# Gated DeltaNet layer on one core: decay matrices and gate vectors spread over the partitions by DMA from DRAM, in place of TensorE transposes

## The chip, the cores and the metric

The kernel runs on one core of a Trainium2 chip. The metric is the device time of one execution in microseconds, as the median of several runs.

## What is computed

One decoder layer in float32, over 256 positions of width 2048: a gated DeltaNet token mixer and a SwiGLU channel mixer, each followed by a layer norm, with gates, scales and shifts from a conditioning vector `c`. The mixer has 16 query/key heads and 32 value heads of width 128. The reference, cut to the parts near the change:

```python
mod = (cond @ mod_w[i] + mod_b[i])[:, None, :]
sh1, sc1, ga1, sh2, sc2, ga2 = jnp.split(mod, 6, axis=-1)
h = x * (1 + sc1) + sh1
y = gated_deltanet(h, ...)
x = layer_norm(ALPHA_DN * x + (1 + ga1) * y, ln_g[i, 0], ln_b[i, 0])
h = x * (1 + sc2) + sh2
y = swiglu(h, ffn_w_gu[i], ffn_w_down[i])
x = layer_norm(ALPHA_DN * x + (1 + ga2) * y, ln_g[i, 1], ln_b[i, 1])

# in the mixer, per chunk and head
g = -jnp.exp(a_log) * jax.nn.softplus(a + dt_bias)
gc = jnp.cumsum(g, -1)
diff = gc[..., :, None] - gc[..., None, :]
decay = jnp.where(lower, jnp.exp(jnp.where(lower, diff, 0.0)), 0.0)
L = jnp.where(strict, jnp.einsum('bhnid,bhnjd->bhnij', kb, k) * decay, 0.0)
sol = lax.linalg.triangular_solve(L + I, rhs, left_side=True, lower=True, unit_diagonal=True)
a_qk = jnp.where(lower, jnp.einsum('bhnid,bhnjd->bhnij', q, k) * decay, 0.0)
```

The kernel works with two chunks of 128 positions (c = 0, 1).

## The kernel before

**The products.** Every large product is split in three: each weight tile is divided into a high part `wh` (ScalarE, L190) and a low part `wl` (VectorE, L191), the activations likewise, and TensorE runs three 128x512 products per pair of tiles (L223 to L225). A `Group` makes 512 output columns; a `chunk` of it is four row tiles of the weight for both halves of the positions, 24 products. `pos` counts chunks, and all times of the plan ("units") are in chunks. Weights come by DMA through the queue of SyncE (SP).

**The stages.** First the conditioning scales `sc1`, `sh1` and the transposed, scaled input `hT` are made while the first projections already run. Then the projections of q/k, v and z follow, quarter by quarter (`q` = 0 to 3; a quarter is four query/key heads and eight value heads). Then w_out, the first layer norm (`ln1`), the feed-forward products (w_gu, then w_down) and the last norm.

**Tasks beside the stream.** The mixer's own work is written as generators. `spawn(t, gen)` puts one on a heap at plan time t, `advance` runs whatever is due and gives its instructions the priority of that time; a `yield d` moves the task d units on. The language's planner then orders the instructions of each engine by these priorities and by its own estimate of when operands are ready. On the chip each engine runs its queue in that fixed order. The constants in lines 35 to 39 are such distances.

**The mixer of a quarter.** `gates` (L410) makes `beta` and the cumulated log decays `gc` (positions on partitions, a column for each chunk and head), `ngc` = -gc and the exponentials. `qk_done` and `v_done` spawn the convolutions; `v_done` of the second half also spawns `gdn(q)`. `gdn` waits until q's norms are there and until the states of quarter q-1 are done (`state_ends`), takes the tile `LA` (one buffer, 128 x 16 x 2 x 128: for each chunk and head the matrix of the solve and the matrix a_qk), and spawns four `la_task`s. Each handles one chunk and four heads:

- ScalarE writes `dg` = gc of a head down the columns plus a matrix `below` of -1e30 under the diagonal (L543), four Identity activations of 128x128;
- TensorE transposes it (L547, four transposes into a `gd` PSUM buffer);
- ScalarE makes the decay `dm` = Exp(transpose + ngc) (L551);
- TensorE makes the k.k and k.q products `pk` (L556), and VectorE multiplies them by `dm` and the row scales into LA (L561).

`solve_task` then inverts the triangular matrices in place (VectorE's long loop, then products of LA's blocks), and `state_task` runs the two chunks through the state; its last operation is L686. `dg` and `dm` share the tag `V` (3 buffers) with the state's tiles.

**The tail of the mixer.** When a quarter's states end, `fo` follows (a `pow` on GpSimd, L718), z's gate is applied (L795), and `o_task` transposes and splits the results into the operands `oT` of w_out (L817, L818). These take the places of tiles that have become free: `oTa` those of `kq`, `oTb` that of `LA`, and so on.

**Gate vectors.** `gate_row` (L831) turns a gate, held as 128 x 16 columns (`ga1`, `ga2`), into a row of 2048 on all partitions: for each column a TensorE transpose of the broadcast column (L838), 16 in all, and four ScalarE copies (L839). It is called for `ga1` ahead of w_out and for `ga2` ahead of w_down; `residual` reads the row (L845). `mods_late` makes `ga1` and `ga2` from streamed weights (`macc`, L272).

GpSimd's queue holds few instructions: the `pow` for `rn` and `fo`, a MEMSET and a COPY that prepare X of the solve, and the DMAs of small or repeated tensors.

Of the kernel before, what the change touches and what calls it, by code (L numbers as in the profile page):

```python
# [8 lines left out]
F32 = mybir.dt.float32  # L9
# [7 lines left out]
D = 2048  # L17
# [12 lines left out]
def gdn_layer_kernel(ctx: ExitStack, tc: tile.TileContext, x, c, mod_w, mod_b, ln_g, ln_b,  # L30
# [7 lines left out]
    GDN, LAGAP, LA1, LA2, LA3, SOLVE, HOP = 3.0, 0.5, 0.3, 0.6, 1.5, 5.4, 0.6  # L38
# [82 lines left out]
    below = consts.tile([128, 128], F32, name="below")  # L121
    ts(below, jp, 0.0, -1e30, op0=OP.is_gt, op1=OP.mult)
# [282 lines left out]
    negc = consts.tile([128, 32], F32, name="negc")  # L405
    XN = gp.tile([64, 16, 64], F32, name="XN", tag="XN", bufs=1)
# [3 lines left out]
    def gates(ps):  # L410
# [37 lines left out]
        ts(ngc, gc, -1.0, None, op0=OP.mult)  # L448
        act(egc, gc[:, 1, :], AF.Exp)
# [5 lines left out]
    oq, fo, LA, omq, state_done, state_ends = {}, {}, {}, {}, {}, set()  # L455

# [78 lines left out]

    def la_task(q, c, g, sc):

        kqq, hv, la = kq[q], q * 8, LA[q]
        s0 = c * 8 + g * 4
        dg = gp.tile([128, 4, 128], F32, name="dg", tag="V", bufs=3)  # L540
        for i in range(4):
            h = hv + g * 4 + i
            act(dg[:, i, :], below, AF.Identity, bias=gc[:, c, h:h + 1])  # L543
        yield LA1
        pb = gd()
        for i in range(4):
            tr(pb[:, i * 128:(i + 1) * 128], dg[:, i, :], ident)  # L547
        dm = gp.tile([128, 4, 128], F32, name="dm", tag="V", bufs=3)
        for i in range(4):
            h = hv + g * 4 + i  # L550
            act(dm[:, i, :], pb[:, i * 128:(i + 1) * 128], AF.Exp, bias=ngc[:, c, h:h + 1])  # L551
        yield LA2
        pk = gd()
        for n in range(2):
            nn = g * 2 + n
            mm(pk[:, n * 256:(n + 1) * 256], kqq[:, nn, 0, c * 128:(c + 1) * 128],  # L556
               kqq[:, nn, :, c * 128:(c + 1) * 128], start=True, stop=True)
        for i in range(4):
            h = g * 4 + i
            src = pk[:, (i // 2) * 256:(i // 2 + 1) * 256].rearrange("p (a b) -> p a b", a=2)  # L560
            stt(la[:, s0 + i], src, sc[:, 0, c, h:h + 1], dm[:, i, None, :].to_broadcast([128, 2, 128]),  # L561
                op0=OP.mult, op1=OP.mult)

# [127 lines left out]
    def gdn(q):  # L691


        while q not in rq2 or q and q - 1 not in state_ends:
            yield 0.2
        hv, rk, rq = q * 8, rk2[q], rq2[q]
        LA[q] = gp.tile([128, 16, 2, 128], F32, name="LA", tag="LA", bufs=1)
# [3 lines left out]
        tt(sc[:, 1, 0], sc[:, 0, 0], kse[:, hv:hv + 8], op=OP.mult)  # L701
        for c in range(2):
            for g in range(2):
                spawn(now[0] + LAGAP * (2 * c + g), la_task(q, c, g, sc))
# [24 lines left out]
    def qk_done(q, which):  # L729
        nat = []  # L730

        def done(t, ps, n=None):
            nat.append(evac(t, ps) if n is None else n)
            if t == 0:
                return
            both = []
            ss = work.tile([128, 2, 4], F32, name="ss", tag="ss", bufs=2)
            t1 = conv_start()
            for h in (0, 2):
                spawn(t1 + PAIR / 2 * h, qk_pair(q, which, nat, h, ss, both))  # L740
            spawn(t1 + PAIR + SILU + 0.6, qk_norm(q, which, ss, both))
        return done
# [88 lines left out]
    def gate_row(tag, cols, name):  # L831

        row = held.tile([128, D], F32, name=name, tag=tag)
        for g in range(4):
            p = tp()
            for i in range(4):
                k = 4 * g + i
                tr(p[:, i * 128:(i + 1) * 128], cols[:, k:k + 1].to_broadcast([128, 128]), ident)  # L838
            act(row[:, g * 512:(g + 1) * 512], p, AF.Copy)  # L839
# [58 lines left out]
    with at(n - 4):  # L898
# [7 lines left out]
        gates(pp)  # L906

# [216 lines left out]
```

## Time and profile before

| | us |
|---|---|
| median of the runs shown | 1728.11 (three runs, 1725.67 to 1729.37) |
| the profiled execution's own time | 1724.8 |
| span of the profile, first to last instruction | 1723.0 |
| TensorE busy | 1668.4 |
| VectorE busy | 1140.0 |
| ScalarE busy | 879.3 |
| GpSimd busy | 49.0 |

In the profile PE is TensorE, PEld its weight loads, DVE is VectorE, ACT ScalarE, POOL GpSimd and SP SyncE; a trailing q is an engine's queue. A line such as L547 is a line of the kernel before. "out<-in" names the tile that is written and those that are read. Records of products overlap, because the array is pipelined, so the sum of their durations is more than the time they take. "Idle before" is time for which the engine waited ahead of an instruction, with what ended it.

### The profile page before, as it was taken

Reading aid. Unit: us, or ns where it says so; the run is one execution under the profiler, and the core shown is the slowest. Engines: PE = TensorE matmul, PEld = TensorE weight load, DVE = VectorE, ACT = ScalarE, POOL = GpSimd, SP = SyncE. Lnnn points to the kernel's source line nnn. Section 1 sums busy time; section 2 is a strip of 40 time slices with the busy share of each in tenths; the row PEclk is TensorE's granted clock in tenths of the full one; section 3 lists DMA queues with packets and bytes.
Section 4 is the critical chain, followed back from the end, with each engine's and each line's share of the span. In section 5 each row is a group of like instructions: output and inputs, shape, how many; then the busy total and the mean of one; then the engine's idle time right before and its main releaser. Section 6 shows DMA issues by size and latency. Waiting matters only on the chain.

```text
span 1723.0 us, 23257 instructions
## 1 busy us (share of the span) xinstructions
PE 1668.4 (97%) x8685; PEld 1325.3 (77%) x8685; DVE 1140.0 (66%) x1641; ACT 879.3 (51%) x1426; POOL 49.0 (3%) x58
## 2 busy tenths in 40 slices
PE   5999999999999999999999999999999999999996
PEld 2666777787887878787788778888878887888885
DVE  2466988958966988847776865764567444455455
ACT  2433669769568667564333734444444443433331
POOL 0000000001001000000000000000000000000000
PEclk8999999999999999999999999999999999999998
DMA  9998785535863777747888576886678666765653
GB/s 351 364 337 282 225 290 186 171 111 160 257 205 112 245 247 240 247 147 237 300 285 278 159 259 193 298 271 188 187 243 290 186 190 204 249 195 190 196 193 107
DMA packets 183938, 390.82 MB, mean 227 GB/s; under 512 B 12096, under 2 KB 14320, under 8 KB 182800
## 3 DMA queue, kind: packets, MB, share of 16 engines
q1 hardware_dynamic: 181808, 378.64, 67.5%
q0 software_dynamic: 2016, 10.68, 1.8%
q8 instruction: 68, 1.11, 0.3%
q14 instruction: 46, 0.38, 0.1%
HBM read 385.08 MB, written 4.19 MB: 226 GB/s over the span
## 4 chain that ended last, share of the span: by engine, by line
PE 71%; DVE 11%; DMA 8%; issue 5%; ACT 3%; POOL 1%; SPq 1%; DVEq 0%; POOLq 0%; ACTq 0%
PE pj L224 19%; PE pj L223 19%; PE pj L225 19%; DMA mraw<-in_mod_w_dram 6%; DVE wl L191 5%; DVE macc L272 1%; PE gd L225 1%; PE gd L224 1%; ACT wh L190 1%; PE gd L223 1%; PE tp L311 1%; DVE X L586 1%; DVE cy L470 1%; DVE tmp L584 1%; PE tp L1039 1%
## 5 line engine op out<-in xcount | busy, mean ns | idle before, releaser
L191 DVE TENSOR_TENSOR wl<-raw,wh 128x1024 fp32r<-128x1024 f32 x522 | 634.9, 1222 | 375.5 <-ACT wh L190 372.4
L190 ACT ACTIVATE wh<-raw 128x1024 fp32r<-128x1024 f32 x522 | 552.3, 1061 | 603.2 <-PE pj L225 480.9
L223 PE MATMUL pj<-wh,h2T 128*128 128x512 f32 x704 | 278.2, 395 | 0.0
L225 PE MATMUL pj<-wh,h2T 128*128 128x512 f32 x704 | 276.7, 393 | 0.0
L224 PE MATMUL pj<-wl,h2T 128*128 128x512 f32 x704 | 276.6, 393 | 0.0
L223 PE MATMUL pj<-wh,hT 128*128 128x512 f32 x640 | 256.9, 403 | 0.0
L224 PE MATMUL pj<-wl,hT 128*128 128x512 f32 x640 | 256.4, 401 | 0.1
L225 PE MATMUL pj<-wh,hT 128*128 128x512 f32 x640 | 256.2, 401 | 0.0
L272 DVE SCALAR_TENSOR_TENSOR macc<-mraw,cond,macc 128x1024 f32<-128x1024 f32 x120 | 153.4, 1278 | 55.8 <-DMA mraw<-in_mod_w_dram 55.4
L223 PEld LDWEIGHTS pj<-wh,h2T 128*128 128x128 f32 x704 | 132.8, 189 | 30.7 <-issue 1.6
L225 PEld LDWEIGHTS pj<-wh,h2T 128*128 128x128 f32 x704 | 132.7, 189 | 28.6 <-issue 0.8
L224 PEld LDWEIGHTS pj<-wl,h2T 128*128 128x128 f32 x704 | 132.7, 188 | 27.5 <-issue 0.8
L223 PEld LDWEIGHTS pj<-wh,hT 128*128 128x128 f32 x640 | 120.8, 189 | 26.6 <-issue 3.3
L225 PEld LDWEIGHTS pj<-wh,hT 128*128 128x128 f32 x640 | 120.9, 189 | 24.6 <-issue 1.2
L224 PEld LDWEIGHTS pj<-wl,hT 128*128 128x128 f32 x640 | 120.8, 189 | 24.4 <-DVE wl L191 0.9
L470 DVE SCALAR_TENSOR_TENSOR cy<-tp,cw,cy 128x255 f32<-128x255 f32 (+2 forms) x192 | 86.2, 476 | 1.3 <-ACT cy L466 1.2
L224 PE MATMUL gd<-wl,hT 128*128 128x512 f32 x128 | 51.5, 404 | 1.4 <-DVE wl L191 1.4
L223 PE MATMUL gd<-wh,hT 128*128 128x512 f32 x128 | 49.9, 398 | 2.0 <-DVE part L256 1.1
L225 PE MATMUL gd<-wh,hT 128*128 128x512 f32 x128 | 51.8, 408 | 0.0
L311 PE MATMUL tp<-mraw,cond 128*32 128x256 f32 x368 | 34.9, 464 | 11.1 <-DMA mraw<-in_mod_w_dram 11.1
L223 PE MATMUL pj<-wh,oTc 128*128 128x512 f32 x112 | 43.9, 392 | 0.0
L225 PE MATMUL pj<-wh,oTc 128*128 128x512 f32 x112 | 43.8, 391 | 0.0
(385 smaller groups left out, 2252.0 us busy)
## 6 DMA issues: line engine op xcount, KB each, us to landing
raw<-in_gdn_w_in_dram SPq DMA_DIRECT2D x194, 512.0 KB, 4.7
mraw<-in_mod_w_dram SPq DMA_DIRECT2D x192, 512.0 KB, 5.4
raw<-in_ffn_w_gu_dram SPq DMA_DIRECT2D x176, 512.0 KB, 4.4
raw<-in_ffn_w_down_dram SPq DMA_DIRECT2D x88, 512.0 KB, 4.7
raw<-in_gdn_w_out_dram SPq DMA_DIRECT2D x64, 512.0 KB, 5.0
x<-in_x_dram SPq DMA_DIRECT2D x8, 256.0 KB, 6.0
r<-in_x_dram POOLq DMA_DIRECT2D x2, 1024.0 KB, 5.1
x1s<-r POOLq DMA_DIRECT2D x2, 1024.0 KB, 6.7
```

Source lines behind the costliest of these rows:

```text
L190: act(hi, raw, AF.Copy)
L191: tt(lo, raw, f32(hi), op=OP.subtract)
L223: mm(ps, sh, wh, start=start, stop=False)
L224: mm(ps, sh, wl, start=False, stop=False)
L225: mm(ps, sl, wh, start=False, stop=stop)
L272: return stt(acc, w, cond[:, k:k + 1], acc, op0=OP.mult, op1=OP.add)
L311: mm(p[32 * j:32 * j + 32, 0:hw], cond[:, k:k + 1].to_broadcast([128, 32]), raw[:, kl, j * hw:(j + 1) * hw], start=(k == 0), stop=(k == KT ...
L470: stt(y[:, o + s:o + 256], p[:, o:o + 256 - s], tap(3 - s, ct + i), y[:, o + s:o + 256], op0=OP.mult, op1=OP.add)
L584: tt(tv, LD[:, j + 1:32, j:j + 1].to_broadcast([128, n, m]), X[:, j, None, 0:m].to_broadcast([128, n, m]), op=OP.mult)
L586: tt(X[:, j + 1:32, 0:m], X[:, j + 1:32, 0:m], tv, op=OP.subtract)
L1039: tr(p[:, i * 256 + t * 128:i * 256 + (t + 1) * 128], nats[j, t][:, (2 * i2 + i) * 128:(2 * i2 + i + 1) * 128], ident)
```

## The change

The decays come by another way. After `gc` is made, `gates` transposes it once (64 rows of 128: chunk and head by position), copies it to SBUF and writes it to a DRAM scratch `gcrows` by a DMA on the GpSimd queue. A new task `decay_task(q)`, spawned when q's second q/k group is done, waits for the end of the states of quarter q-1 and for the gates, takes the tile LA, and issues four DMAs on the GpSimd queue. Each reads four rows of `gcrows` and spreads them over all 128 partitions, straight into the a_qk half of LA. After LA1 units GpSimd masks each block in place (`affine_select`, -1e30 under the diagonal), and ScalarE applies the Exp in place, with `ngc` as bias. `la_task` keeps the products and the multiplication, which now reads the decay from LA itself; `dg`, its transposes, `dm` and `below` are gone. `gdn` waits for the first decay block of its quarter before it spawns the `la_task`s. The distances LA1, LA2 and LA3 change.

`gate_row` transposes the 128 x 16 columns once, copies 16 rows of 128 to SBUF, writes them to a DRAM scratch and reads them back as a row of 2048 on all 128 partitions; both DMAs are on the GpSimd queue.

```diff
--- before.py
+++ after.py
@@ -35,7 +35,7 @@
     SPLIT, MOD0, MODEVERY = 10, 30.0, 0.95
     MGAP, CGAP0, CGAP, CSTEP = 1.5, 1.0, 2.0, 2.3
     CONV, PAIR, SILU = 0.2, 0.4, 2.4
-    GDN, LAGAP, LA1, LA2, LA3, SOLVE, HOP = 3.0, 0.5, 0.3, 0.6, 1.5, 5.4, 0.6
+    GDN, LAGAP, LA1, LA3, SOLVE, HOP = 3.0, 0.5, 1.2, 0.8, 5.4, 0.6
     ALONE, MACW, ZW, OW = 1.5, 1.0, 0.1, 0.3
 
 
@@ -118,8 +118,6 @@
     ones = upper[:, 127:128]
     mhalf = consts.tile([128, 16], F32, name="mhalf")
     nc.vector.memset(mhalf, -0.5)
-    below = consts.tile([128, 128], F32, name="below")
-    ts(below, jp, 0.0, -1e30, op0=OP.is_gt, op1=OP.mult)
 
     pbit = work.tile([128, 1], I32, name="pbit", tag="gw0", bufs=1)
     nc.gpsimd.iota(pbit, pattern=[[0, 1]], base=0, channel_multiplier=1)
@@ -403,6 +401,7 @@
     ngc = consts.tile([128, 2, 32], F32, name="ngc")
     egc = consts.tile([128, 32], F32, name="egc")
     negc = consts.tile([128, 32], F32, name="negc")
+    gcrows = dram.tile([64, 128], F32, name="gcrows", tag="gcrows", bufs=1)
     XN = gp.tile([64, 16, 64], F32, name="XN", tag="XN", bufs=1)
     nc.gpsimd.memset(XN[0:32, :, 32:64], 0.0)
     kse = consts.tile([128, 32], F32, name="kse")
@@ -446,6 +445,12 @@
         mm(p[:, 64:96], ones.to_broadcast([128, 128]), q[:, 0, :], start=True, stop=True)
         nc.vector.tensor_copy(gc, p[:, 0:64].rearrange("p (a b) -> p a b", a=2))
         ts(ngc, gc, -1.0, None, op0=OP.mult)
+
+        pr = tp()
+        tr(pr[:64, 0:128], gc.rearrange("p a b -> p (a b)"), ident)
+        gr = work.tile([64, 128], F32, name="gr", tag="hf", bufs=2)
+        nc.vector.tensor_copy(gr, pr[:64, 0:128])
+        nc.gpsimd.dma_start(gcrows, gr)
         act(egc, gc[:, 1, :], AF.Exp)
         ts(negc, egc, -1.0, None, op0=OP.mult)
         tt(kse, p[:, 64:96], gc[:, 0, :], op=OP.subtract)
@@ -453,6 +458,7 @@
 
     kq, knat, rk2, rq2, ik2 = {}, {}, {}, {}, {}
     oq, fo, LA, omq, state_done, state_ends = {}, {}, {}, {}, {}, set()
+    has_gates, has_decay = [], set()
 
     def conv_silu(nat, h, ct, dst):
 
@@ -533,23 +539,29 @@
                 act(oq[q][:, c, hq + i, :], p[:, c * 256 + i * 128:c * 256 + (i + 1) * 128], AF.Copy,
                     scale=ik2[q][:, c, hq + i:hq + i + 1])
 
+    def decay_task(q):
+
+        while q and q - 1 not in state_ends or not has_gates:
+            yield 0.2
+        LA[q] = gp.tile([128, 16, 2, 128], F32, name="LA", tag="LA", bufs=1)
+        parts = [(c, g, LA[q][:, c * 8 + g * 4:c * 8 + g * 4 + 4, 1, :]) for c in range(2) for g in range(2)]
+        for c, g, dm in parts:
+            h0 = c * 32 + q * 8 + g * 4
+            nc.gpsimd.dma_start(dm, gcrows[None, h0:h0 + 4, :].to_broadcast([128, 4, 128]))
+        yield LA1
+        for c, g, dm in parts:
+            nc.gpsimd.affine_select(dm, dm, pattern=[[0, 4], [1, 128]], compare_op=OP.is_ge, fill=-1e30,
+                                    base=0, channel_multiplier=-1)
+            for i in range(4):
+                h = q * 8 + g * 4 + i
+                act(dm[:, i, :], dm[:, i, :], AF.Exp, bias=ngc[:, c, h:h + 1])
+            has_decay.add(q)
+            yield LAGAP
+
     def la_task(q, c, g, sc):
 
-        kqq, hv, la = kq[q], q * 8, LA[q]
+        kqq, la = kq[q], LA[q]
         s0 = c * 8 + g * 4
-        dg = gp.tile([128, 4, 128], F32, name="dg", tag="V", bufs=3)
-        for i in range(4):
-            h = hv + g * 4 + i
-            act(dg[:, i, :], below, AF.Identity, bias=gc[:, c, h:h + 1])
-        yield LA1
-        pb = gd()
-        for i in range(4):
-            tr(pb[:, i * 128:(i + 1) * 128], dg[:, i, :], ident)
-        dm = gp.tile([128, 4, 128], F32, name="dm", tag="V", bufs=3)
-        for i in range(4):
-            h = hv + g * 4 + i
-            act(dm[:, i, :], pb[:, i * 128:(i + 1) * 128], AF.Exp, bias=ngc[:, c, h:h + 1])
-        yield LA2
         pk = gd()
         for n in range(2):
             nn = g * 2 + n
@@ -558,8 +570,10 @@
         for i in range(4):
             h = g * 4 + i
             src = pk[:, (i // 2) * 256:(i // 2 + 1) * 256].rearrange("p (a b) -> p a b", a=2)
-            stt(la[:, s0 + i], src, sc[:, 0, c, h:h + 1], dm[:, i, None, :].to_broadcast([128, 2, 128]),
+            stt(la[:, s0 + i], src, sc[:, 0, c, h:h + 1], la[:, s0 + i, None, 1, :].to_broadcast([128, 2, 128]),
                 op0=OP.mult, op1=OP.mult)
+        return
+        yield
 
     def solve_task(q):
 
@@ -691,14 +705,15 @@
     def gdn(q):
 
 
-        while q not in rq2 or q and q - 1 not in state_ends:
+        while q not in rq2 or q not in LA:
             yield 0.2
         hv, rk, rq = q * 8, rk2[q], rq2[q]
-        LA[q] = gp.tile([128, 16, 2, 128], F32, name="LA", tag="LA", bufs=1)
         sc = work.tile([128, 2, 2, 8], F32, name="gsc", tag="gsc", bufs=2)
         tt(sc[:, 0], rk, rk, op=OP.mult)
         tt(sc[:, 0], sc[:, 0], beta[:, :, hv:hv + 8], op=OP.mult)
         tt(sc[:, 1, 0], sc[:, 0, 0], kse[:, hv:hv + 8], op=OP.mult)
+        while q not in has_decay:
+            yield 0.1
         for c in range(2):
             for g in range(2):
                 spawn(now[0] + LAGAP * (2 * c + g), la_task(q, c, g, sc))
@@ -739,6 +754,8 @@
             for h in (0, 2):
                 spawn(t1 + PAIR / 2 * h, qk_pair(q, which, nat, h, ss, both))
             spawn(t1 + PAIR + SILU + 0.6, qk_norm(q, which, ss, both))
+            if which == 1:
+                spawn(t1, decay_task(q))
         return done
 
     def v_done(q, half):
@@ -831,12 +848,13 @@
     def gate_row(tag, cols, name):
 
         row = held.tile([128, D], F32, name=name, tag=tag)
-        for g in range(4):
-            p = tp()
-            for i in range(4):
-                k = 4 * g + i
-                tr(p[:, i * 128:(i + 1) * 128], cols[:, k:k + 1].to_broadcast([128, 128]), ident)
-            act(row[:, g * 512:(g + 1) * 512], p, AF.Copy)
+        p = tp()
+        tr(p[:KT, 0:128], cols, ident)
+        rows = work.tile([KT, 128], F32, name="grow", tag="rows", bufs=2)
+        nc.vector.tensor_copy(rows, p[:KT, 0:128])
+        there = dram.tile([KT, 128], F32, name=f"{name}d", tag=name, bufs=1)
+        nc.gpsimd.dma_start(there, rows)
+        nc.gpsimd.dma_start(row, there.rearrange("k p -> (k p)")[None, :].to_broadcast([128, D]))
         return row
 
     def residual(row, g, t, ps, xin, st):
@@ -904,6 +922,7 @@
             mm(pp, wl, hh, start=False, stop=False)
             mm(pp, wh, hl, start=False, stop=(k == KT - 1))
         gates(pp)
+        has_gates.append(True)
 
     def late_mods():
         yield from mods_late(ga1, 32, 1.0, MODEVERY)
```

## Rows read from the trace of the kernel before

**Rows 1.** The page's head: span, then busy time, share and instructions of each engine.
```profile
span 1723.0 us, 23257 instructions
...
PE 1668.4 (97%) x8685; PEld 1325.3 (77%) x8685; DVE 1140.0 (66%) x1641; ACT 879.3 (51%) x1426; POOL 49.0 (3%) x58
```

**Rows 2.** Busy us by stretches: length, PE, PEld, DVE, ACT, POOL, clock, DMA share, GB/s.
```profile
258.00:301.00 43.00, 42.99 (x211) 34.39 (x210) 35.09 (x60) 42.70 (x92) 0.00 (x0) 1.00 0.60 190
...
516.00:559.00 43.00, 41.56 (x220) 33.45 (x219) 29.45 (x64) 37.01 (x104) 4.54 (x2) 1.00 0.40 118
...
1118.00:1161.00 43.00, 43.00 (x194) 35.28 (x193) 28.09 (x26) 18.40 (x20) 0.00 (x0) 1.00 0.83 278
```

**Rows 3.** Groups of instructions of TensorE and ScalarE: busy us, mean ns, idle before.
```profile
L547 PE MATMUL gd<-ident,dg 128*128 128x128 f32 x64 | 15.4, 278 | 0.0
...
L838 PE MATMUL tp<-ident,ga 128*128 128x128 f32 x32 | 4.6, 276 | 0.1
...
L543 ACT ACTIVATE dg<-below,gc 128x128 f32<-128x128 f32 x64 | 21.3, 407 | 0.0
L551 ACT ACTIVATE dm<-gd,ngc 128x128 f32<-128x128 f32 x64 | 19.0, 372 | 1.1 <-PE gd L547 1.0
```

**Rows 4.** Timeline of TensorE around one block of transposes: start, length.
```profile
250.88 0.39 PE L225 MATMUL pj<-wh,hT 128*128 128x512 f32 x1
251.11 0.60 PE L547 MATMUL gd<-ident,dg 128*128 128x128 f32 x4
...
251.78 0.40 PE L224 MATMUL pj<-wl,hT 128*128 128x512 f32 x1
```

**Rows 5.** Timeline of VectorE: quarter 0's decays and LA, then quarter 2's LA.
```profile
241.22 0.23 DVE L447 COPY gc<-tp 128x64 f32<-128x64 f32 x1 [0.79 <-PE tp L446]
...
278.58 1.65 DVE L561 SCALAR_TENSOR_TENSOR LA<-gd,gsc,dm 128x256 f32<-128x256 f32 x4
...
524.81 0.69 DVE L686 TENSOR_TENSOR oq<-gd,Qs 128x512 f32<-128x512 f32 x1 [1.94 <-PE gd L685]
...
532.57 1.66 DVE L561 SCALAR_TENSOR_TENSOR LA<-gd,gsc,dm 128x256 f32<-128x256 f32 x4 [0.74 <-PE gd L547]
...
541.86 1.65 DVE L561 SCALAR_TENSOR_TENSOR LA<-gd,gsc,dm 128x256 f32<-128x256 f32 x4
```

**Rows 6.** DMA issues: count, size of each, median us from issue to landing.
```profile
x1s<-r POOLq DMA_DIRECT2D x2, 1024.0 KB, 6.7
...
lrow<-in_ln_g_dram POOLq DMA_DIRECT2D x1, 1024.0 KB, 5.1
...
l<-in_ln_g_dram POOLq DMA_DIRECT2D x4, 256.0 KB, 8.6
```

**Rows 7.** Groups of GpSimd's instructions.
```profile
L509 POOL TENSOR_TENSOR rn<-ss,mhalf 128x8 f32<-128x8 f32 x8 | 15.2, 1894 | 233.7 <-DVE ss L507 196.0 <-DVE gsc L701 37.6
...
L578 POOL COPY X<-parity 128x16 f32<-128x16 f32 x8 | 2.8, 383 | 0.3
...
L1093 POOL DMA_DIRECT2D l<-in_ln_g_dram x4 | 2.1, 539 | 0.0
L576 POOL MEMSET X<- 128x512 f32 x4 | 2.1, 527 | 163.5 <-PE gd L610 160.0 <-PE tp L462 3.5
```

**Rows 8.** Timeline: w_out's first operand in LA's place is made, then read.
```profile
768.88 0.75 DVE L818 SCALAR_TENSOR_TENSOR oTb<-tp,nwc,oTb 128x512 fp32r<-128x512 f32 x1
...
781.12 0.48 PE L223 MATMUL pj<-wh,oTb 128*128 128x512 f32 x1
```

**Rows 9.** Instructions on the tile ga1row: ns min/median/max, first and last start.
```profile
L845 DVE TENSOR_TENSOR ry<-pj,ga1row x8: 680/684/691, 819.5 to 958.0; 128x512 f32<-128x512 f32 x8
L839 ACT ACTIVATE ga1row<-tp x4: 580/594/598, 791.3 to 794.5; 128x512 f32<-128x512 f32 x4
```

**Rows 10.** Timeline of VectorE and GpSimd from 422.9 us.
```profile
422.95 1.28 DVE L272 SCALAR_TENSOR_TENSOR macc<-mraw,cond,macc 128x1024 f32<-128x1024 f32 x1
423.12 2.61 POOL L509 TENSOR_TENSOR rn<-ss,mhalf 128x8 f32<-128x8 f32 x1 [10.26 <-DVE ss L507]
```

## The prediction

> **What bounds the kernel now.** The first view to open is the head of the page [rows 1]. The reader is to see that TensorE is busy 1668.4 of 1723.0 us, and that no other engine comes near it. A share over the whole span hides stages with other limits, so the second view is the busy time by stretches of 43 us [rows 2]. In the stretch from 258 us, where the first of the four quarters of heads is worked on, ScalarE is busy 42.70 of 43 us and TensorE 42.99. In the stretch from 516 us TensorE is busy 41.56 and ScalarE 37.01, with the DMA engines at 0.40. From 1118 us, in the feed-forward part, TensorE has no idle time at all. So the product stream on TensorE sets the pace in all stages that the change touches: an instruction taken out of that stream shortens the time by its place in the stream, and an instruction taken from another engine is worth nothing unless TensorE was waiting for it. All of TensorE's idle time is 1723.0 - 1668.4 = 54.6 us.
>
> **What a transpose costs in the stream.** The change takes out two groups of TensorE transposes, 64 of `dg` (L547) and 32 of the gate columns (L838). A record of one lasts about 0.276 us [rows 3], but records overlap, so that is not its price. The timeline shows the price [rows 4]: the product before a block of four starts at 250.88, the second product after it at 251.78, so 0.90 us hold two products and four transposes. A product alone takes 43.00 / 194 = 0.222 us (TensorE's row of the stretch from 1118, where nearly all instructions are such products). That leaves 0.90 - 0.444 = 0.456 us for four, 0.114 us for one.
>
> **The change, part by part.**
> *Removed in `la_task`.* 64 transposes: 64 x 0.114 = 7.3 us of stream. 64 Identity activations take 21.3 us of ScalarE [rows 3]; I count them at nothing, because even in the stretch from 258 us, with ScalarE full, TensorE idles only 0.01 us [rows 2]. The transposes also leave two uses of the `gd` PSUM buffers and of the `V` buffers; nothing in the rows shows TensorE waiting for these, so nothing is counted. The 64 Exp activations stay and read SBUF in place of PSUM; I take them as unchanged.
>
> *Removed in `gate_row`.* 32 transposes: 32 x 0.114 = 3.6 us. Eight ScalarE copies of about 0.59 us [rows 9] go too; they are hidden beside products.
>
> *Added on TensorE.* One transpose in `gates` and one in each `gate_row`: 3 x 0.114 = 0.3 us. Net of the stream: 7.3 + 3.6 - 0.3 = 10.6 us.
>
> *Added: gate vectors through DRAM.* A small write, then a 1 MB broadcast read. Nearest rows [rows 6]: 6.7 us for the 1 MB write of `x1s`, 5.1 us for the 1 MB broadcast of `ln_g`. Together at most 12 us. The vector used to begin at 791.3 and is first read at 819.5 [rows 9], 28 us later, so this lies under w_out's products; the second one, ahead of w_down, has the same kind of cover. Cost zero; without the cover it would be these 12 us once each.
>
> *Added: the decay path.* Once: a copy and a small DRAM write in `gates`. For each quarter: four DMA issues on the GpSimd queue, each spreading 4 rows of 512 B to 128 partitions (256 KB), four masks `affine_select` of 128x512 on GpSimd, then the Exps. For quarter 0 the sums `gc` are there at 241.22 and LA is first written at 278.58 [rows 5]: 37 us of cover, for a write of at most 6.7 us, a read of 5.1 to 8.6 us [rows 6] and the masks. It costs nothing there. Quarter 1 has no tight start either, because `gdn(1)` is spawned by the values' projection and not by the end of quarter 0.
>
> Quarters 2 and 3 are the tight ones: LA has one buffer, so the DMAs can start only when the states of the quarter before have read it. Before, states end at 524.81 + 0.69 = 525.5, LA is written from 532.57, and the last block from 541.86 [rows 5]: 16.4 us from free buffer to last block. After: four issues of 0.54 us (the `l` row of [rows 7]) are 2.2 us; landing takes 5.1 to 8.6 us, and I take the 8.6 of the rows with several 256 KB broadcasts issued together [rows 6], as here; then four masks of m each in a row, then four Exps of 0.372 us [rows 3], 1.5 us. In all 12.3 + 4m against 16.4: late by 4m - 4.1 us. No row shows a mask. Below it stands the MEMSET of the same 128x512, 0.527 us; above it the COPY of 16 strided columns, 0.383 us or 24 ns a column, which would make 12.3 us of 512 columns [rows 7]. I take m = 1 us, near the MEMSET, since the shape is the same and only a read is added. Then the path is as early as before (0.1 us), and the sum has no loss.
>
> What is queued behind these waits: on GpSimd the `pow` for `fo` and `rn` and the MEMSET of X; on VectorE, behind the first L561 that waits for a decay, the `wl` splits on which every product depends; on ScalarE, behind an Exp that waits for a mask, the `wh` splits. So a decay that is really late doesn't stay beside the stream, it stops it. The dues also move: LA1 is now 1.2 units after the states' end, and LA3 falls from 1.5 to 0.8, which puts the solve 0.7 unit earlier where the decays are ready in time, and about 0.6 later for quarters 2 and 3. At the very end there is cover: the first operand of w_out that takes LA's place is complete at 768.88 + 0.75 = 769.6, and TensorE reads it at 781.12 [rows 8], 11.5 us later; past that, a late quarter 3 would stop w_out.
>
> *Added DMA bytes.* 16 x 256 KB and 2 x 1 MB are 6 MB; in the stretch from 516 us the DMA engines are busy 0.40 of the time, so the weights keep their lead. The longer GpSimd work is 16 masks on an engine busy for 49.0 us in all [rows 1].
>
> **The sum.** 1724.8 us is the profiled execution's own time (span 1723.0 and 1.8 around it). 1724.8 - 10.6 = 1714.2. The median of the runs shown, 1728.1, lies 3.3 above that execution, so the forecast for a median is 1728.1 - 10.6 = 1717.5.
>
> **A rule weighed.** GpSimd's `pow` for `rn` that starts at 423.12, inside VectorE's `macc` of 422.95 to 424.23, lasts 2.61 us against a mean of 1.894 [rows 7, 10]: a GpSimd operation that meets a VectorE operation with two SBUF inputs is longer by 0.7 us or more. The Trainium skill ("SBUF — State Buffer", section "SBUF: two separate sides") says that the port pair which the two engines share is locked by whichever starts first for the whole instruction, against a VectorE operation with two SBUF inputs too, and that the other one is blocked until then. By that rule each mask can wait out one VectorE operation, and the time would be the second rival's 1727.5 in place of 1717.5; the row agrees as far as GpSimd's side goes, and no row here shows VectorE held.
>
> **The rivals.**
> *Larger gain (chance 0.09).* The transposes are worth the busy time that their rows show, and not their place: 15.4 + 4.6 = 20.0 us [rows 3], less three new ones (0.7 us), 19.3 us: 1708.8. For it: ScalarE full at 258 us. Against it: the 0.90 us of [rows 4].
>
> *Masks and VectorE hold each other (0.14).* Each mask waits out one `macc` of 1.28 us [rows 10]: m = 2.28 us, late by 4 x 2.28 - 4.1 = 5.0 us in each of two quarters, 10.0 us together. Nearly all the gain is eaten: 1727.5, no change that can be told. For it: the 2.61 us. Against it: in the stretch from 516 us VectorE is busy 29.45 of 43 us [rows 2], and many of its operations there read PSUM.
>
> *Slower, by late decays in quarters 2 and 3 (0.15).* The same wait with a mask of 3.5 us or a landing that is as much later: 4 x 3.5 - 4.1 = 9.9 us twice, 19.8 us: 1717.5 + 19.8 = 1737. It decides from 2 x (4m - 4.1) = 10.6, that is from m = 2.4 us. For it: one buffer for LA, and VectorE's and ScalarE's queues in fixed order. Against it: the MEMSET. At the far end, 12.3 us a mask, it would be 2 x 45.1 = 90 us.
>
> **The numbers.** The forecast case (net 10.6 us, 1714 to 1722) has 0.62. A measurement of this kernel can tell about 0.2%, 3.5 us, from no change, so "same" is 1724.6 to 1731.6. Faster is the forecast and the larger gain, 0.71; same 0.14; slower 0.15. The range for 8 in 10 runs from 1709 (the larger gain) to 1730 (past the rival that eats the gain); most of the slower case lies outside.
>
> **What would show it.** L547 and L543 are gone, three transposes stand in place of L838's 32, and TensorE has about 10 us less of busy and idle time together. `affine_select` lasts about 1 us, its DMA 5 to 9. From the states' end to the last LA block of quarters 2 and 3 it is about 16 us, and no wait of VectorE or ScalarE on a decay is longer than 2 us. The prediction is wrong if the masks take over 2.4 us, if `wl` or `wh` comes late behind a decay, or if TensorE waits for the first operand in LA's place in w_out.

## The result and the profile after

The changed kernel takes 1739.79 us (median of 4 runs, 1737.03 to 1743.26) against 1728.44 for the kernel before: ratio 1.0079, 95% interval 1.0052 to 1.0106, so it is slower by 9 to 18 us. The forecast was 1717.5.

The profiled execution took 1737.03 us. First its page's head, beside [rows 1]:

```profile
span 1735.3 us, 23071 instructions
...
PE 1664.0 (96%) x8592; PEld 1321.5 (76%) x8592; DVE 1145.6 (66%) x1643; ACT 854.9 (49%) x1350; POOL 74.0 (4%) x95
```

TensorE's busy time fell by 4.4 us, its idle time rose from 54.6 to 1735.3 - 1664.0 = 71.3 us, by 16.7. That is the whole difference of the spans, 12.3 us: work was taken out of the stream, and more than it was worth came back as stops. (Busy time also counts products that run at the lower clock, so the 4.4 us is not the price of what was taken out.) The busy time by stretches (columns as in [rows 2]) shows where:

```profile
258.00:301.00 43.00, 39.77 (x198) 31.98 (x197) 39.97 (x68) 40.48 (x91) 2.48 (x4) 1.00 0.65 194
387.00:430.00 43.00, 38.37 (x188) 30.68 (x188) 31.73 (x60) 31.77 (x90) 10.81 (x10) 0.96 0.48 144
516.00:559.00 43.00, 41.23 (x205) 33.32 (x204) 26.74 (x47) 34.76 (x97) 10.12 (x10) 1.00 0.42 123
645.00:688.00 43.00, 35.81 (x164) 29.12 (x163) 31.08 (x52) 25.38 (x60) 8.45 (x9) 0.92 0.60 195
```

These are the four places where a quarter's decays are made and used. Before, TensorE was busy 42.99 and 41.56 us in the first and third [rows 2]; the second and fourth were:

```profile
387.00:430.00 43.00, 42.84 (x220) 33.37 (x219) 35.01 (x71) 40.05 (x118) 7.15 (x3) 1.00 0.51 160
645.00:688.00 43.00, 42.08 (x207) 34.46 (x206) 38.38 (x66) 30.65 (x73) 2.90 (x1) 1.00 0.75 236
```

So TensorE lost 3.2, 4.5, 0.3 and 6.3 us in quarters 0 to 3: quarter 2 lost next to nothing. In the worst stretch, from 645 us, it is busy 35.81 us, and the granted clock is 0.92. The waits of the changed kernel name the instruction that is stopped, and what VectorE stands on meanwhile (in all us, times, longest us):

```profile
DVE fo L734 <- POOL fo L733: 15.6, 4, 7.6
PE gd L568 <- DVE LA L573: 15.6, 4, 7.0
```

L568 are the products of `la_task` that write `pk`, L573 the multiply that reads `pk` and the decay. `fo` is the factor of a finished quarter's normalisation: GpSimd raises 16 columns to the power -0.5 (L733), VectorE multiplies the result (L734). Before, VectorE's wait there was a third:

```profile
DVE fo L719 <- POOL fo L718: 5.1, 3, 3.0
```

Of the new operations only the DMA issues cost more than assumed (0.764 us each instead of 0.54): GpSimd's groups, then the DMA issues' landings (columns as in [rows 6]).

```profile
L733 POOL TENSOR_TENSOR fo<-ft,mhalf 128x16 f32<-128x16 f32 x4 | 12.6, 3142 | 0.9 <-DVE ft L732 0.9
L550 POOL DMA_DIRECT2D LA<-gcrows x16 | 12.1, 764 | 99.5 <-PE gd L699 62.9 <-ACT knat L503 33.0 <-DMA raw<-in_gdn_w_in_dram 3.6
L553 POOL TENSOR_SCALAR_AFFINE_SELECT LA<-LA 128x512 f32<-128x512 f32 x16 | 11.0, 694 | 8.7 <-DMA LA<-gcrows 8.6
```

```profile
LA<-gcrows POOLq DMA_DIRECT2D x16, 256.0 KB, 5.8
...
ga1row<-ga1rowd POOLq DMA_DIRECT2D x1, 1024.0 KB, 8.4
...
gcrows<-gr POOLq DMA_DIRECT2D x1, 32.0 KB, 3.5
```

The timeline of quarter 3's start, behind two lines each of quarters 1 and 2, shows how they hold TensorE (start, length, engine, line):

```profile
397.80 2.40 POOL L553 TENSOR_SCALAR_AFFINE_SELECT LA<-LA 128x512 f32<-128x512 f32 x4
...
398.39 1.25 DVE L730 TENSOR_TENSOR ft<-rr 128x16 f32<-128x16 f32 x1
...
537.72 2.95 POOL L733 TENSOR_TENSOR fo<-ft,mhalf 128x16 f32<-128x16 f32 x1
540.65 1.25 POOL L553 TENSOR_SCALAR_AFFINE_SELECT LA<-LA 128x512 f32<-128x512 f32 x2
...
659.37 2.15 PE L568 MATMUL gd<-kq 128*128 128x256 f32 x8
659.64 0.69 DVE L700 TENSOR_TENSOR oq<-gd,Qs 128x512 f32<-128x512 f32 x1 [0.88 <-PE gd L699]
660.07 3.04 POOL L550 DMA_DIRECT2D LA<-gcrows  x4 [31.55 <-PE gd L699]
...
664.26 0.17 DVE L732 TENSOR_SCALAR ft<-ft 128x16 f32<-128x16 f32 x1
...
665.06 0.64 POOL L553 TENSOR_SCALAR_AFFINE_SELECT LA<-LA 128x512 f32<-128x512 f32 x1 [1.96 <-DMA LA<-gcrows]
...
665.74 1.28 ACT L557 ACTIVATE LA<-LA,ngc 128x128 f32<-128x128 f32 x4 [2.79 <-POOL LA L553]
...
667.05 0.39 PE L221 MATMUL pj<-wh,hT 128*128 128x512 f32 x1
...
668.45 0.63 POOL L553 TENSOR_SCALAR_AFFINE_SELECT LA<-LA 128x512 f32<-128x512 f32 x1 [0.46 <-DMA LA<-gcrows]
...
669.05 2.94 POOL L733 TENSOR_TENSOR fo<-ft,mhalf 128x16 f32<-128x16 f32 x1
671.96 0.63 POOL L553 TENSOR_SCALAR_AFFINE_SELECT LA<-LA 128x512 f32<-128x512 f32 x1
672.02 0.60 DVE L734 TENSOR_TENSOR fo<-fo,rr 128x16 f32<-128x16 f32 x1 [7.59 <-POOL fo L733]
672.54 0.16 DVE L730 TENSOR_TENSOR ft<-rr 128x16 f32<-128x16 f32 x1
...
672.63 3.21 DVE L573 SCALAR_TENSOR_TENSOR LA<-gd,gsc,LA 128x256 f32<-128x256 f32 x8
...
674.42 2.05 PE L568 MATMUL gd<-kq 128*128 128x256 f32 x4 [6.99 <-DVE LA L573]
...
676.58 1.66 DVE L573 SCALAR_TENSOR_TENSOR LA<-gd,gsc,LA 128x256 f32<-128x256 f32 x4 [0.73 <-PE gd L568]
...
677.12 0.63 PE L221 MATMUL pj<-wh,hT 128*128 128x512 f32 x1
677.54 0.63 PE L222 MATMUL pj<-wl,hT 128*128 128x512 f32 x1
...
679.40 0.88 DVE L573 SCALAR_TENSOR_TENSOR LA<-gd,gsc,LA 128x256 f32<-128x256 f32 x2 [1.17 <-PE gd L568]
```

Read it engine by engine. TensorE sends the first two blocks' products at 659.37, right behind the quarter's end; they fill both `gd` buffers. 26 weight products follow, then the third block's products, which need a buffer: TensorE stands from 667.4 to 674.4. The first block's decay is ready at 665.74 + 1.28 = 667.0. But VectorE, in its order, is to run L734 first. Its operand was ready for the power at 664.4, and GpSimd is at the masks, of which each waits for a landing; the power starts at 669.05, behind the third. Of VectorE's 7.59 us of wait, 4.6 pass before the power starts, and the rest is the power itself. So the first L573 starts at 672.63, 5.6 us after its decay. And after the stop, products start 0.42 us apart (677.12, 677.54), where 0.22 is usual: the granted clock is 0.55 from 675 to 679 us, so for most of that time TensorE runs at the lower of its two levels, 1.2 GHz. Of the stretch's 43 us, the 0.08 that the granted clock lacks is 3.4 us. The runs show it as well: the mean granted clock of the change is 0.989 (4 runs), of the kernel before 0.993 (the 17 runs beside the first experiments). By an estimate from these shares and the spans, the lower clock is worth some 7 us.

The power stands behind masks in quarter 3 alone. In quarter 2 (537.72) and in quarter 1 it runs ahead of them, right behind the four issues: there VectorE's waits of 3.7 and 2.8 us are mostly the power's own length, and the masks come after it.

Here one rule of the Trainium skill can be set beside rows again ("SBUF — State Buffer", section "SBUF: two separate sides": VectorE and GpSimd share a port pair, and whichever starts first can lock the other out). While four masks run from 397.80 to 400.20, VectorE's 128x16 product at 398.39 lasts 1.25 us; the same line lasts 0.16 at 672.54. L734 at 672.02 lasts 0.60 us, about as long as the mask beside it (671.96). The trace agrees, this time on VectorE's side. The masks were hardly held: median 0.634 us of 16, one of 1.607.

### The profile page after: what moved, and what is told of

Same layout as the page of the kernel before. It is cut to its first block, busy times and chain, and to the rows that moved or that the text cites. A ratio compares the mean times of both kernels' runs of the same rounds, so it can differ in the third digit from the quotient of the medians.

```text
span 1735.3 us, 23071 instructions
## 1 busy us (share of the span) xinstructions
PE 1664.0 (96%) x8592; PEld 1321.5 (76%) x8592; DVE 1145.6 (66%) x1643; ACT 854.9 (49%) x1350; POOL 74.0 (4%) x95
## 4 chain that ended last, share of the span: by engine, by line
PE 72%; DVE 11%; DMA 6%; issue 6%; ACT 3%; POOL 1%; SPq 1%; DVEq 0%; POOLq 0%; ACTq 0%
PE pj L223 19%; PE pj L222 19%; PE pj L221 19%; DMA mraw<-in_mod_w_dram 5%; DVE wl L189 4%; PE gd L223 2%; PE gd L222 1%; PE gd L221 1%; DVE macc L270 1%; PE tp L309 1%; ACT wh L188 1%; DVE X L600 1%; DVE tmp L598 1%; DVE cy L476 1%; PE gd L568 1%
```

## Experiments

Every kernel has its own line numbers: the products of `la_task`, L568 in the change, are L565 without the DMAs, and the multiplies L573 are then L570. The expectations call these products "the products of A", after the matrix A that they fill in LA, and they name their theories by letters, of which A is another one:

- A: the first two blocks hold both `gd` buffers until their decays come, so the third block's products wait.
- B: a late decay stops the stream through the `wl` and `wh` queued behind it.
- C: masks, landings and exponentials cost by being there.
- Q: the power is queued on GpSimd behind masks that wait for landings.
- L: the decay is late by itself.
- P: the products stand right behind the quarter's end, so that their multiplies meet the power and what follows it on VectorE.
- W: VectorE, in its order, stands waiting for the power, with the multiplies behind.

**The two parts alone.** One kernel is the one before with the new `gate_row`; the other is the changed kernel with the old `gate_row`.

> The kernel before with the new gate_row alone (the decays stay with TensorE). All theories agree: the stream loses 32 transposes and gains two, 30 x 0.114 = 3.4 us, and the DRAM round trip lies under the products. Expected 3 to 4 us faster than before (ratio 0.998); if the round trip is late for residual, slower than before.

> The changed kernel with the old gate_row, so the decays' way alone. All theories agree that the loss is here: 12 us of the whole change plus the 3 to 4 us that gate_row gives, 15 to 16 us slower than before (ratio 1.009). If it is under 8 us slower, the loss needs both parts.

Measured: the rows alone 1721.99 (ratio 0.9978, 0.9964 to 0.9991), the decays alone 1746.66 (1.0116, 1.0096 to 1.0136). The rows gain about 4 us, as priced; all of the loss, and more, is in the decays: 20 us, where 15 to 16 were expected. The wait of L568 on L573 is 17.9 us in the latter.

**Free the buffers at once.** ScalarE copies `pk` from PSUM to SBUF, and L573 reads the copy:

```diff
+        pks = gp.tile([128, 512], F32, name="pks", tag="V", bufs=3)
+        act(pks, pk, AF.Copy)
-            src = pk[:, ...
+            src = pks[:, ...
```

> The changed kernel, with one more ScalarE copy per block: pk goes from PSUM to a V buffer at once, and VectorE multiplies from there, so a late decay holds V buffers (three) and not the two gd buffers. Theory A (TensorE's third pk product waits because the first two blocks hold both gd buffers until their decays come, 15.6 us of stops in four quarters, and some 5 us at half the clock after them): TensorE's waits for L573 are gone, 18 to 20 us faster than the changed kernel, about 1720. Theory B (the late decay stops the stream anyway, through wl and wh behind the waiting L573 and Exp): the stop moves to VectorE or ScalarE, 1735 or more. Theory C (masks and DMAs contend with VectorE and the weights): no change but for 16 copies, 1740.

1737.31 (1.0064, 1.0048 to 1.0081), as theory B had it. The stops at these products went, and others of 2.2 to 3.4 us took their place, most of them at transposes and weight products behind late VectorE and ScalarE work. So freeing the buffers, at the price of 16 copies on ScalarE, gives next to none of the time back.

**Decays early, products late.** In the first kernel the decays of quarters 1 to 3 are made in other tiles, from the end of the solve before; in the second, the products L568 get a lower priority, so that the first of them stand 28 to 38 weight products behind the quarter's end; the third has both.

```diff
-        while q and q - 1 not in state_ends or not has_gates:
+        while q and q - 1 not in solved or not has_gates:
...
+            with at(now[0] + (0, 5., 10., 13.)[q]):
                 mm(pk[:, n * 256:(n + 1) * 256], ...
```

> The changed kernel, with the decays of quarters 1 to 3 put in the tiles LD, X and diag, which are free once the quarter before is solved: their DMAs start some 30 us sooner and no longer wait for LA. Theories A and B agree: the decays are there when the states end, the stops of quarters 1 to 3 go (4.6 + 7.0 + some 2 us and the half clock after them), 14 to 20 us faster than the changed kernel, 1720 to 1726, and about 5 us or more below before. Theory C: the same masks and the same bytes run beside the same work, no gain, about 1738.

> Changed kernel with the products of A of quarters 1 to 3 put later in TensorE's order, by their priority alone: the first stand some 28 to 38 weight products (6 to 9 us) behind the quarter's end and the third some 52 to 61 (12 to 14 us) behind it, where the changed kernel has 0 and 24 to 35; their DMAs, masks and exponentials stay where they are. Q, L and P: TensorE has products to run while the decay comes, the stops at the products of A go, and the time is 1722 to 1727, the chain of the quarters being a little longer (the end of quarter 3's states moves from 32 weight products ahead of the output projection to about its start). Theory C (masks, landings and exponentials cost by being there): no gain, 1736 to 1742.

> The kernel with early decays (in tiles of their own, from the end of the solve of the quarter before), with the products of A of quarters 1 to 3 put later in TensorE's order in the same way. P: what was lost was the place of the products alone; with early decays and late products neither is left: 1718 to 1724. Q: the power and the clearing of the solve's start are still queued on GpSimd behind masks that wait for landings (37.8 us of its idle time), beside the solve: about 1740. L expects no more than the kernel with early decays gave, unless the products' place counts: 1740 to 1748.

1748.30 (1.0120, 1.0101 to 1.0139), 1741.49 (1.0096, 1.0077 to 1.0116) and 1746.59 (1.0120, 1.0099 to 1.0141): none gained. Theory C fits the second (1736 to 1742) and theory L the third (1740 to 1748); the first is above every range. VectorE's timeline of the first, at quarter 1's start, shows one reason why an early decay was not enough:

```profile
399.08 1.27 DVE L580 SCALAR_TENSOR_TENSOR LA<-gd,gsc,DM 128x256 f32<-128x256 f32 x3 [0.24 <-PE gd L575]
...
404.01 0.18 DVE L744 TENSOR_TENSOR fo<-fo,rr 128x16 f32<-128x16 f32 x1 [2.66 <-POOL fo L743]
404.10 0.48 DVE L580 SCALAR_TENSOR_TENSOR LA<-gd,gsc,DM 128x256 f32<-128x256 f32 x1
```

The multiplies (here L580) start with no wait for a decay, and then stand behind the power. That isn't all. This kernel's order is another one: the third block's products stand 6 to 11 weight products behind the second's, where the change has 24 to 35. And between the quarters' starts (the stretches from 301, 430 and 559 us, 86 us each) TensorE idles 12.7 us, against 5.4 in the change. So the run doesn't show what an early decay alone is worth.

With late products VectorE waits as long for the power (14.0 us in all), and TensorE stops at other places; that these stops come from the power isn't shown:

```profile
PE gd L569 <- DVE LA L574: 5.5, 2, 3.9
PE tp L468 <- ACT tp L507: 5.3, 4, 2.2
PE tp L801 <- DVE X L601: 3.7, 1, 3.7
PE pj L222 <- DVE wl L189: 3.5, 3, 2.2
```

So two suspects are left: the landings on GpSimd's queue, and the power in the same queue.

**Landings and power, each taken away.** Without landings: the masks read a resident tile (the decays are then other numbers). Without the power: VectorE multiplies instead (the normalisation is then another). The last is the control, the kernel before with the new rows and without the power.

```diff
-            nc.gpsimd.dma_start(dm, gcrows[None, h0:h0 + 4, :].to_broadcast([128, 4, 128]))
-            nc.gpsimd.affine_select(dm, dm, ...
+            nc.gpsimd.affine_select(dm, upper[:, None, :].to_broadcast([128, 4, 128]), ...
...
-        nc.gpsimd.tensor_tensor(f..., t..., mhalf, op=OP.pow)
+        tt(f..., t..., mhalf, op=OP.mult)
```

> Changed kernel without the DMAs of the decays: the mask reads a resident tile of zeros and ones and writes the place of A, and Exp takes gc itself as its bias, so the decays are not the reference's; the scratch is written and not read. Nothing lands late, and GpSimd never stands in front of a landing. Theory Q (the masks wait for the landings on GpSimd, the power for the normalisation of the quarter before is queued behind them, 7.6 us of VectorE's wait in quarter 3, and the multiplies of A behind that): all of the 18 us of TensorE's stops are back, about 1721. Theory L (the decay is late by itself, whatever is queued): the same, about 1721. Theory P (the products of A stand right behind the quarter's end in TensorE's order, so their multiplies meet the power and its followers on VectorE whenever the decay is there; the kernel with early decays lost 2.5 to 2.9 us at each of three borders so): stops of about 2.5 us a border stay, 1728 to 1734.

> Changed kernel with a multiply on VectorE in place of the power, so that its normalisation is not the reference's; DMAs, masks and exponentials of the decays are as in the changed kernel. It is the fourth of four: landings and power (the change, 1739.8), no landings (1728.8), neither (1717.5), and this, landings alone. If both matter by themselves, and add up: 1739.8 less 11 is 1726 to 1731, quarter 3's multiplies of A starting at about 667 instead of 672.6. If the power costs only where nothing else is late, or the landings hold the multiplies as long: 1735 to 1740.

> The kernel without the decays' DMAs, and with a multiply on VectorE in place of the power, so that its normalisation is not the reference's either. Neither a landing nor a power is waited for. W: the stops of 2.5 to 2.9 us that were left at the products of A at each border go, 1718 to 1722, which is the sum of the prediction (1717.5). P (the products collide with the quarter's end in any case): 1726 to 1730.

> Control: the kernel before with the new gate rows and a multiply on VectorE in place of the power, so that its normalisation is not the reference's. In the kernel before no stop of TensorE hangs on the power: 1720 to 1723, as with the rows alone. If it comes to 1717, the 1717.5 of the kernel with neither landing nor power is owed to the power that is gone, and not to the transposes.

| kernel | us | ratio to before | 95% interval |
|---|---|---|---|
| the change | 1739.79 | 1.0079 | 1.0052 to 1.0106 |
| without landings | 1728.80 | 1.0018 | 1.0003 to 1.0032 |
| without the power | 1731.59 | 1.0035 | 1.0023 to 1.0048 |
| without both | 1717.48 | 0.9963 | 0.9947 to 0.9978 |
| control: before, new rows, no power | 1718.58 | 0.9963 | 0.9950 to 0.9977 |

The landings are worth 0.0061 with the power and 0.0072 without it, 10 to 12 us; the power 0.0044 and 0.0055, 8 to 10 us. By the intervals each of these differences is good to 0.002 to 0.003, 3.5 to 5 us, so within that they add up, and with both gone the kernel is below the one before. Of the recorded ranges, theory P's fits the kernel without landings (1728 to 1734, where Q and L had about 1721); the one without the power came out at the upper end of the sum expected (1726 to 1731), and the one without both just under theory W's 1718 to 1722. The edit takes the issues and the bytes away together with the landings, and doesn't part them. ScalarE's wait for the projections' weights hardly moves, though: 24.8 us before, 27.1 in the change, 27.7 without landings, so nothing points to the bytes. In the kernel before the power is worth 0.0015 by the medians (control against the rows alone), within the intervals. Without landings, VectorE still stands on each of four powers, and the products of A behind it:

```profile
DVE fo L731 <- POOL fo L730: 11.3, 4, 3.1
PE gd L565 <- DVE LA L570: 7.5, 3, 2.7
```

Without the power, VectorE waits for the decay itself, and TensorE's stops at these products shrink from 15.6 to 8.2 us, half of it in quarter 0:

```profile
PE gd L568 <- DVE LA L573: 8.2, 3, 4.1
...
DVE LA L573 <- ACT LA L557: 4.1, 4, 1.9
```

Without both, one stop is left there:

```profile
PE gd L565 <- DVE LA L570: 0.5, 1, 0.5
```

Every one of these kernels has an order of its own. In quarters 1 to 3 the third block's products stand 35, 24 and 26 weight products behind the second's in the change, and 41, 30 and 23 with both gone: 6 later in two quarters (1.3 us each) and 3 earlier in one, too little to explain 20 us. The rest of the orders wasn't compared.

**The product behind the power moved to GpSimd.** One edit that keeps the results: GpSimd does L734 itself. It was run on the changed kernel, with late products too, and on the kernel before with the new rows.

```diff
-        tt(f, f, rq, op=OP.mult)
+        nc.gpsimd.tensor_tensor(f, f, rq, op=OP.mult)
```

> Changed kernel, where the product behind the power for the normalisation of a quarter is done by GpSimd, right behind the power, and no longer by VectorE. Theory W: VectorE, in its order, stands on that product for the power (15.6 us in the changed kernel, of them 7.6 in quarter 3 and 3.7 in quarter 2, against 5.1 in all before), with the multiplies of A that free the products' buffers queued behind it; so in quarters 2 and 3 the multiplies start when the decay is there (quarter 3 at about 667 instead of 672.6), TensorE's stops there fall from 7.2 and 1.7 to 1 to 2, and quarter 1 stays, since the next reader of the power stands ahead of the multiplies there: 1731 to 1735. Theory L (the landings alone): the decay is as late as before, 1738 to 1741.

> The same, and the products of A of quarters 1 to 3 later in TensorE's order (as in the kernel with late products, which gained nothing by that). W: there it was VectorE's wait for the power (14.0 us) that stopped TensorE at whatever came next; without it the late products give what they were to give: 1725 to 1732. If the late products lengthen the chain of the quarters, and that is the loss: 1738 to 1742.

> The kernel before, with the new gate rows and with the product behind the power on GpSimd. The kernel before waits 5.1 us for powers on VectorE and no wait of TensorE names what is queued behind them, so W expects no more than from the rows alone: 1720 to 1723; if the power holds TensorE there too, 1717 to 1720.

1740.19 (1.0089, 1.0068 to 1.0109), 1738.25 (1.0079, 1.0055 to 1.0102) and 1719.51 (0.9970, 0.9954 to 0.9987). On the change it did nothing, where theory W expected 1731 to 1735: the wait only moved, to the next reader of `fo` (5.4 us) and to the next writer of `ft`, the power's operand, which has one buffer. The line of the latter, and the next wait for a power in the same queue, on VectorE's timeline of quarter 2:

```profile
544.09 0.89 DVE L730 TENSOR_TENSOR ft<-rr 128x16 f32<-128x16 f32 x1 [3.74 <-POOL fo L733]
...
547.26 0.60 DVE L518 TENSOR_SCALAR rr<-rn 128x16 f32<-128x16 f32 x1 [1.75 <-POOL rn L515]
```

So the edit doesn't take VectorE's wait away, and theory W is neither borne out nor refuted by it. On the kernel before it gives the lowest time of those that compute the reference; it can't be told from the rows alone, 0.9978.

**The price of a transpose.** Without landings and power the changed kernel is only level with its control, although 64 transposes are gone. In one kernel (before, with the new rows) each of these is done twice; in the other (without landings and power) the masks are left out too.

```diff
-        for i in range(4):
-            tr(pb[:, i * 128:(i + 1) * 128], dg[:, i, :], ident)
+        for i in range(8):
+            tr(pb[:, i % 4 * 128:(i % 4 + 1) * 128], dg[:, i % 4, :], ident)
```

> The kernel before with the new gate rows, where each of the 64 transposes of the decays is done twice. The prediction's price (0.114 us of TensorE's stream each): 7.3 us more than the rows alone, 1728 to 1731. If they lie beside other waits and cost nothing: 1720 to 1724.

> The kernel without landings and without the power, and now without the masks too (the exponentials read the resident tile, so the decays have no mask). The 16 masks are the last of the change's work on GpSimd. If they hold VectorE at the port, or delay the exponentials, so that the gain of the transposes was eaten: 1711 to 1714. If not: 1716 to 1719, as with them.

Doubled: 1738.22 (1.0073, 1.0058 to 1.0089), 16 us over the rows alone, more than twice the price. Without masks: 1716.72 (0.9951, 0.9935 to 0.9967), no difference from 0.9963 that can be told, so in this kernel the masks cost nothing by being there (theory C). The doubled transposes also moved other instructions in the written-out orders, and part of the 16 us are new stops (one of 2.2 us, of a product L556 behind VectorE), so the run gives no clean price; it does show that transposes in this stream are not free.

## Why the prediction was wrong

*Price of the gate rows:* right. 32 transposes for two were forecast at some 3.4 us; the rows alone gained 4.1 us by medians (1.6 to 6.2 by the interval), and their DMAs stayed hidden, as forecast.

*The durations of the decay path:* off, but not to its harm. Issue 0.764 us instead of 0.54, landing 5.8 instead of 8.6, mask 0.694 instead of 1. In quarter 3 the last decay is ready at 672.62 + 1.28 = 673.90, 13.6 us after the buffer is free (659.64 + 0.69 = 660.33), with a power among the masks; the forecast was 12.3 + 4 = 16.3.

*The step that failed* is what was made of this: "Then the path is as early as before (0.1 us), and the sum has no loss." The sum had 0 for the way through DRAM and GpSimd's queue; the runs show 20 us, 10 to 12 for the landings and 8 to 10 for the power in the same queue (1.0079 - 0.9963 = 0.0116 together; 0.0015 of that, inside the noise, the power may have cost before as well). The path was compared by its last block and by quarter 2 alone. From the free buffer to the start of the multiplies, by VectorE's timelines (L686 and L561 before, L700 and L573 after), it is:

| us | before: first block | last block | changed: first block | last block |
|---|---|---|---|---|
| quarter 1 | 9.1 | 19.1 | 10.9 | 30.4 |
| quarter 2 | 7.1 | 16.4 | 6.9 | 14.5 |
| quarter 3 | 8.0 | 17.3 | 12.3 | 19.1 |

For quarter 2 the forecast was right, and TensorE lost 0.3 us there. In quarter 3 the first block's multiplies come 4.3 us later, although its decay is ready 6.7 us after the free buffer: the power holds them, and without the power they come 7.6 us after it. (Quarter 1's last block stands behind convolution work in VectorE's order; without landings it comes at 27.9 us, so that is mostly the order.)

What stops the stream is when TensorE asks, and this, too, was set aside: "The transposes also leave two uses of the `gd` PSUM buffers and of the `V` buffers; nothing in the rows shows TensorE waiting for these, so nothing is counted." Quarter 3 before:

```profile
657.90 0.60 PE L556 MATMUL gd<-kq 128*128 128x256 f32 x2
...
658.34 0.38 PE L547 MATMUL gd<-ident,dg 128*128 128x128 f32 x2
...
660.35 1.65 DVE L561 SCALAR_TENSOR_TENSOR LA<-gd,gsc,dm 128x256 f32<-128x256 f32 x4
...
662.15 0.67 PE L556 MATMUL gd<-kq 128*128 128x256 f32 x2 [0.92 <-DVE LA L561]
```

The transposes took the same two buffers in turn with the products, so the second block's products went out when the first block was multiplied. Without them two blocks go out at the quarter's end and hold both buffers until L573, 8 to 13 us later, and the third stands in TensorE's order 24 to 35 weight products on, 5 to 8 us. This is read from the timelines. The two kernels that attack it, with copies and with late products, gained next to nothing, so how much of the loss hangs on it isn't shown.

*The queue behind the waits* was named ("on GpSimd the `pow` for `fo`") and not priced. In quarter 3 VectorE waits 7.6 us for it, 4.6 of them before it starts.

*Quarters 0 and 1 were thought safe.* For quarter 0 the 37 us of cover went to an earlier due time: its multiplies moved from 278.58 to 254.57, with a stop of 2.4 us. Quarter 1 was said to have "no tight start"; its decay waits for the same buffer of LA, and it has a stop of 4.6 us.

*The signs to watch for* mostly missed it. ScalarE's longest wait for a mask, 2.8 us, is past the 2 us named, but masks last 0.694 us; the longest wait for `wl` is 1.9 us, at 838.67 in w_out; the first operand in LA's place is complete at 779.8 and read at 796.5. A stop at the products of `la_task` was not among them.

*The decays' transposes, 7.3 us:* not borne out. Without landings and power the change is level with its control (difference 0.0000, by both intervals ±0.0020, 3.5 us); without masks too it is 2 us better (±0.0021). In the profiled executions, one each, TensorE is busy 1657.1 us without both and 1667.5 in the control (granted clocks 0.991 and 0.989), and idle 57.4 against 54.5 us: the transposes' time seems to have left its queue (though the control's profiled run, 1723.73, was its slowest). That the medians don't show it, these runs don't settle; small stops that come with another order are a guess.

*The rivals:* "slower, by late decays" had the sign and the size (1737), and the right queues, but wanted a mask of 3.5 us or a later landing, and quarters 2 and 3. The loss came with masks shorter and landings earlier than assumed, and in quarters 0, 1 and 3; the four kernels put it on the landings and the power. Masks and VectorE holding each other is seen only in small (the 1.25 and 0.60 us above).

## What to carry to other kernels

An instruction that is taken out of an in-order engine may have been what paced the next one: look at which buffers they took in turn, and at what will be issued now in its place, before its price is booked as a gain. When a DMA replaces on-chip work, ask which instruction waits for the landing and what unrelated work shares that queue; here it was a 3 us power that another engine needed. A late chain has several links of like length: moving them (buffers, place, early start) gained next to nothing, and taking one away, landings or power, gave half of the loss back.

## What the runs showed of the hardware

A 128x512 `affine_select` on GpSimd lasts 0.63 us (median of 16), near a MEMSET of that shape (0.53). A power on 128x16 lasts 2.9 to 3.8 us there. VectorE's 128x16 products beside a mask last 0.60 to 1.25 us instead of 0.16. Four DMA issues hold GpSimd's queue for 3.04 us. A stop of 7 us on TensorE was followed by products at 0.42 us instead of 0.22 (granted clock 0.55 for 4 us), so a stop costs more than its length.
